# One queue for the first loads, and other priorities and margins for the scheduler of a two-layer decoder trunk

## The chip, the cores and the metric

The kernel runs on one core of a Trainium2 chip (trn2). Five engines work side by side: TensorE (PE in the rows, its weight loads PEld), VectorE (DVE), ScalarE (ACT), GpSimd (POOL) and SyncE (SP, which here only issues DMAs). The metric is the device time of one launch in microseconds (us); lower is better. Three runs of the kernel before took 282.83, 282.81 and 280.10 us, median 282.81 us.

## What is computed

Two layers of a mixer on a residual stream `x` of 256 tokens by 1024 features, all in float32. Cut to what matters:

```python
for l in range(2):
    h = rms_norm(x, g_pre[l]);  u = h @ w_in[l]          # 1024 -> 3344 columns, split into:
    qa, ka, va, ga, qb, kb, vb, gb, rb, qm, gm = split(u)
    oa = causal_attention(norm(qa), norm(ka), va, alibi) * silu(ga)        # 8 heads of 64
    log_a = log_sigmoid(rb @ w_gate_up[l] + b_gate_up[l]) / 16
    ob = rms_norm(gated_linear_attention(qb, kb, vb, log_a)) * silu(gb)    # "GLA", 4 heads, chunks of 64
    mk, mv = split(rms_norm(mem, g_mem[l]) @ w_mem_kv[l])
    om = attention(norm(qm), norm(mk), mv) * silu(gm)                      # 4 heads over 256 memory tokens
    x = x + concat(oa, ob, om) @ w_out[l]
```

## The kernel before

**Numbers in two parts.** A float32 operand is split into a rounded part and a rest (`whi`/`wlo` for weights, `xh`/`xl` for the normalised input, `oh`/`ol` for the gated outputs and, earlier in a layer, for the memory tokens), and each product is three matmuls: high by high, high by low, low by high. The high part is a copy on ACT (line 404 for weights, 345 for the first ones; 259 or, on POOL, 261 for activations), the low part a subtraction on DVE (lines 406, 347, 301).

**Units.** Weights come in granules of 256 columns (1 MB each, 272 columns for `vr`). A layer is a run of units: `vr` and `kq` (what GLA needs), then those of `UNITS[l]` (values, queries and keys, gates, and the memory's `mk`, `mv`), then `o0` to `o3` of the output projection. A unit of one granule is 48 matmuls of 256 columns (line 998); a pair, such as `mk mv`, is 48 of 512 columns (line 1005). These 31 units give 1488 of the 2138 matmuls in the trace, and their order among themselves does not depend on the tables of numbers below. Places on TensorE are told by the count of these big matmuls from the start: `kq` ends at 96, `ga0` at 144, `va0 va1` at 192, `qa0 ka0` at 240, `mk mv` at 288.

**Small work between them.** Between the big matmuls TensorE does transpositions (lines 502, 523, 932), the sums of squares of the norms (438), a broadcast (455) and matmuls that use only a part of the array, "small-tile" work: the gate (530), GLA (686, 692, 614, 621 and, at its end, 732), attention scores (880) and probabilities times values (947). The rests of an attention are on DVE, ACT and POOL: line 482 and 917 are POOL's.

**The order.** Nothing is scheduled on the chip. While the program is built, a planner (`Plan.run`) keeps a clock for each engine; each piece of work is a generator that asks for an engine, a cost, the earliest time and a priority. The planner takes the engine whose next piece could start first, and among the pieces ready on that engine the one of highest priority, and the instructions are written in that order; each engine then works through its list strictly in turn. The big matmuls have priority 0, so small work goes in front of them as soon as the planner's clock says that it is ready. Small-tile work on TensorE is held back by `SLACK` plus `HOLD`:

```python
if eng == "P" and t.mode != "main":
    after += SLACK + (HOLD if t.mode != "full" and self.shape == "full" else 0)
```

**The tables.** `PR` is the priority of each kind of work: `a0`, `a1` the two halves of the causal attention, `m` the memory attention, `v` value evacuations, `qk` query and key evacuations, `vr` the evacuation of the first unit with the gate's chain (`vr_evac`, lines 508 to 545), `gla` the GLA chain, `g` gates. `SPLIT` is the priority of splitting weights that are not yet needed, `MEMPRIO` that of the split of the memory tokens, `FSQ` that of the squares of `x`, `STATS` an extra delay of the matmul of line 438, `WARM` how many matmuls on zeros stand in front of the first real one (line 1035).

**The first loads.** `start_loads` (lines 321 to 338) issues `x` in five pieces and `w0` (the weights of `vr` and `kq`, 528 columns for each of eight k) in five pieces: two of `w0` from ACT's queue, all others from SP's. `LANDS` tells the planner when each piece is there. Behind them come the constants (`cst`), `wup`, and then the other weights, each into one of three raw buffers as one comes free. `first_unit` works through k = 0 to 7, twelve matmuls for each.

## Time and profile before

| | |
|---|---|
| runs | 282.83, 282.81, 280.10 us (median 282.81) |
| the profiled execution | 281.19 us, of which the span (first to last instruction) is 279.4 us |
| TensorE matmul busy | 272.0 us, 97% of the span |
| TensorE weight load busy | 241.1 us, 86% |
| VectorE busy | 229.5 us, 82% |
| ScalarE busy | 193.3 us, 69% |
| GpSimd busy | 89.0 us, 32% |
| chain that ended last | TensorE 87%, VectorE 7%, DMA 2% |

Matmuls overlap one another, so that a row's busy time is longer than the distance from its start to the next start; the distance is what a matmul costs. The chain of work that ended last follows, from the last instruction back, what released each step; its rows add up to the span, and in it a row of matmuls tells the time that passed, not the busy time.

### The profile page before, as it was taken

To read this page: it belongs to the slowest core of one execution; us is meant where nothing else is said; L and a number is where in the kernel's file an instruction comes from. 1 tells how busy PE (TensorE), PEld (TensorE's weight loads), DVE (VectorE), ACT (ScalarE), POOL (GpSimd) and SP (SyncE) were. 2 spreads that over 40 slices of the span, in tenths; PEclk is the share of its full clock that TensorE was granted. 3 is DMA by queue.
4 is the path that set the end of the run, shared out by engine and by line. 5 is a ranking of instruction groups with operands and counts; after the bars stand their busy time and mean duration, and the time that the engine had idled before them with its cause. 6 is when DMAs were issued, how large, how long until landed. Compare 5 with 4: busy or idle time off the path is not lost.

```text
span 279.4 us, 5773 instructions
## 1 busy us (share of the span) xinstructions
PE 272.0 (97%) x2138; PEld 241.1 (86%) x2138; DVE 229.5 (82%) x568; ACT 193.3 (69%) x430; POOL 89.0 (32%) x111
## 2 busy tenths in 40 slices
PE   8899999799999999999999999999999999999994
PEld 7799788487999997999999886789887888989994
DVE  2899799999888898978999798979986787898631
ACT  4874888777797776967773888759787745956400
POOL 3303394160426424400063318213243730510000
PEclk9999999999999999999999999999999999999999
DMA  7999408560734314343545745228233424151111
GB/s 224 402 361 380 175 0 308 198 246 1 289 107 189 103 72 151 122 168 126 201 160 158 287 151 199 104 82 325 63 135 110 192 108 196 50 196 59 56 56 40
DMA packets 8413, 45.76 MB, mean 164 GB/s; under 512 B 945, under 2 KB 2369, under 8 KB 3393
## 3 DMA queue, kind: packets, MB, share of 16 engines
q1 hardware_dynamic: 8096, 44.85, 43.6%
q10 hardware_dynamic: 288, 0.54, 0.7%
q8 instruction: 17, 0.28, 0.4%
q14 instruction: 12, 0.09, 0.1%
HBM read 44.34 MB, written 1.05 MB: 162 GB/s over the span
## 4 chain that ended last, share of the span: by engine, by line
PE 87%; DVE 7%; DMA 2%; ACT 1%; issue 1%
PE bank L998 49%; PE bank L1005 21%; PE bank L947 4%; PE bank L932 3%; PE bank L880 3%; DVE wlo L406 2%; DMA raw<-w_dram 2%; PE bank L502 2%; DVE ol L301 1%; PE bank L732 1%; PE bank L621 1%; DVE sqs L317 1%; ACT L539 0%; PE bank L530 0%; DVE el L581 0%
## 5 line engine op out<-in xcount | busy, mean ns | idle before, releaser
L406 DVE TENSOR_TENSOR wlo<-raw,whi 128x512 fp32r<-128x512 f32 (+1 forms) x144 | 97.8, 700 | 12.0 <-ACT whi L404 10.1
L404 ACT ACTIVATE whi<-raw 128x512 fp32r<-128x512 f32 (+1 forms) x144 | 86.4, 625 | 24.3 <-PE bank L998 11.3
L998 PE MATMUL bank<-xh,whi 128*128 128x256 f32 x160 | 47.1, 294 | 0.0
L998 PE MATMUL bank<-xl,whi 128*128 128x256 f32 x160 | 44.6, 279 | 0.0
L998 PE MATMUL bank<-xh,wlo 128*128 128x256 f32 x160 | 44.6, 279 | 0.0
L917 POOL TENSOR_SCALAR pe<-pe,rc 128x256 f32<-128x256 f32 (+1 forms) x48 | 29.4, 626 | 35.4 <-DVE rc L914 35.2
L998 PE MATMUL bank<-oh,whi 128*128 128x256 f32 x128 | 35.8, 280 | 0.0
L998 PE MATMUL bank<-ol,whi 128*128 128x256 f32 x128 | 35.7, 279 | 0.0
L998 PE MATMUL bank<-oh,wlo 128*128 128x256 f32 x128 | 35.7, 279 | 0.0
L482 POOL TENSOR_TENSOR cc<-ss,nhalf 128x8 f32<-128x8 f32 x12 | 20.5, 1717 | 45.4 <-DVE ss L480 40.9
L1005 PE MATMUL bank<-whi,xh 128*128 128x512 f32 x80 | 32.9, 411 | 0.0
L1005 PE MATMUL bank<-wlo,xh 128*128 128x512 f32 x80 | 31.4, 393 | 0.0
L998 PEld LDWEIGHTS bank<-xh,whi 128*128 128x128 f32 x160 | 30.2, 189 | 1.4 <-issue 1.0
L1005 PE MATMUL bank<-whi,xl 128*128 128x512 f32 x80 | 31.3, 392 | 0.0
L998 PEld LDWEIGHTS bank<-xl,whi 128*128 128x128 f32 x160 | 30.2, 189 | 0.1
L998 PEld LDWEIGHTS bank<-xh,wlo 128*128 128x128 f32 x160 | 30.1, 188 | 0.0
L998 PE MATMUL bank<-whi,xh 128*128 128x256 f32 (+1 forms) x96 | 28.6, 298 | 0.5 <-ACT whi L345 0.5
L998 PE MATMUL bank<-wlo,xh 128*128 128x256 f32 (+1 forms) x96 | 27.6, 288 | 0.5 <-DVE wlo L347 0.4
L998 PE MATMUL bank<-whi,xl 128*128 128x256 f32 (+1 forms) x96 | 27.3, 284 | 0.0
L998 PEld LDWEIGHTS bank<-oh,whi 128*128 128x128 f32 x128 | 24.3, 190 | 0.2 <-issue 0.2
L998 PEld LDWEIGHTS bank<-ol,whi 128*128 128x128 f32 x128 | 24.0, 188 | 0.0
L998 PEld LDWEIGHTS bank<-oh,wlo 128*128 128x128 f32 x128 | 24.0, 188 | 0.0
(188 smaller groups left out, 608.7 us busy)
## 6 DMA issues: line engine op xcount, KB each, us to landing
raw<-win_dram SPq DMA_DIRECT2D x23, 1024.0 KB, 5.3
raw<-wout_dram SPq DMA_DIRECT2D x8, 1024.0 KB, 4.8
raw<-wmkv_dram SPq DMA_DIRECT2D x4, 1024.0 KB, 4.8
raw<-memT_dram SPq DMA_DIRECT2D x2, 1024.0 KB, 4.8
raw<-w_dram SPq DMA_DIRECT2D x3, 528.0 KB, 8.0
raw<-wvr_dram SPq DMA_DIRECT2D x1, 1088.0 KB, 4.9
nb<-nb_dram SPq DMA_DIRECT2D x1, 1024.0 KB, 8.4
out_dram<-xp SPq DMA_DIRECT2D x8, 128.0 KB, 1.9
```

The costliest lines, as they stand in the source:

```text
L301: V.scalar_tensor_tensor(lo[:, k], src[:, k], col(l, g0 + k), hi[:, k].bitcast(F32), op0=ALU.mult, op1=ALU.subtract)
L317: V.tensor_tensor(sqs, sqs, sq[:, j], op=ALU.add)
L404: S.activation(hi[:, cs], raw[:, cs], AF.Copy)
L406: V.tensor_sub(lo[:, cs], raw[:, cs], hi[:, cs].bitcast(F32))
L482: G.tensor_tensor(c, ss, nhalf, op=ALU.pow)
L502: TE.transpose(ps[:, m, tt * P:tt * P + P], n[:, tt, m * P:m * P + P], ident)
L880: TE.matmul(bk[hh][2][:, a:b], lhsT=x[ds], rhs=y[ds], start=(j == 0), stop=(j == len(prs) - 1))
L917: G.tensor_scalar(pe[:, hh, a:b], pe[:, hh, a:b], rc[:, hh, qt:qt + 1], 1.0, op0=ALU.mult, op1=ALU.mult)
L932: TE.transpose(bk[0][2][:, dst:dst + P], pe[:, hh, src:src + P], ident)
L947: TE.matmul(po[64 * hh:64 * hh + 64, q0:T], lhsT=vv[:, j, c:c + 64], rhs=pt[:, hh, 256 * j:256 * j + T - q0], start=(j == 0), stop=(j == 1))
L998: TE.matmul(ps, lhsT=a, rhs=b, start=(first and j == 0), stop=(lastk and j == 2))
L1005: TE.matmul(ps, lhsT=a, rhs=b, start=(first and j == 0), stop=(lastk and j == 2))
```

## The change

The first loads all go to SP's queue, in the order in which `first_unit` uses them (x0, w0, x1, w1, x2-3, w2, w3, x4-5, w4-5, x6-7, w6-7), with six pieces of `w0` where there were five. The dummy matmuls are six where they were five. In the planner the evacuation of the first unit and its gate chain (`vr`) goes from 7 to 9, GLA from 6 to 5, the second half of the causal attention from 8 to 9, the memory attention from 9 to 7, values from 5 to 4, queries and keys from 8 to 7, the split of weights from 6 to 7, the squares of `x` from 6 to 7. `STATS` falls from 800 to 300, `HOLD` rises from 600 to 900. No instruction's kind, shape or engine is changed by hand; the planner makes other lists from these numbers.

```diff
-PR = {'a0': 6, 'a1': 8, 'm': 9, 'v': 5, 'qk': 8, 'vr': 7, 'gla': 6, 'g': 7}
+PR = {'a0': 6, 'a1': 9, 'm': 7, 'v': 4, 'qk': 7, 'vr': 9, 'gla': 5, 'g': 7}
-SPLIT = 6
+SPLIT = 7
-WARM = 5
-FSQ = 6
-STATS = 800
-CHUNKS = ((0, 1), (1, 2), (2, 4), (4, 6), (6, 8))
-LANDS = ((3000, 4200), (4300, 4900), (5600, 6800), (7400, 8500), (9200, 10300))
+WARM = 6
+FSQ = 7
+STATS = 300
+LOADS = (("x", 0, 1, 3100), ("w", 0, 1, 4300), ("x", 1, 2, 4600), ("w", 1, 2, 5300), ("x", 2, 4, 6000),
+         ("w", 2, 3, 6700), ("w", 3, 4, 7600), ("x", 4, 6, 8300), ("w", 4, 6, 9900), ("x", 6, 8, 10600),
+         ("w", 6, 8, 12100))
-SLACK, HOLD = 300.0, 600.0
+SLACK, HOLD = 300.0, 900.0
-        for c, (a, b) in enumerate(CHUNKS):
-            tx, tw = LANDS[c]
-            xs = slice(L * NPRM + a * T if a else 0, L * NPRM + b * T)
-            nc.sync.dma_start(xp[:, xs], xp_d[:, xs])
-            (nc.scalar if b <= 2 else nc.sync).dma_start(raw[:, a:b], src[:, a:b])
-            plan.spawn(first_x(a, b, tx), 30 - 2 * a)
-            plan.spawn(first_w(a, b, tw, raw, hi, lo, got), 29 - 2 * a)
+        for what, a, b, t in LOADS:
+            if what == "x":
+                xs = slice(L * NPRM + a * T if a else 0, L * NPRM + b * T)
+                nc.sync.dma_start(xp[:, xs], xp_d[:, xs])
+                plan.spawn(first_x(a, b, t), 30 - 2 * a)
+            else:
+                nc.sync.dma_start(raw[:, a:b], src[:, a:b])
+                plan.spawn(first_w(a, b, t, raw, hi, lo, got), 29 - 2 * a)
-        yield op("P", 4300, 0.0, None, None, "main")
+        yield op("P", 4700, 0.0, None, None, "main")
```

Line numbers of the changed kernel are one or two higher from line 259 on (998 is 1000, 947 is 949, 261 is 262).

**The start.** SP's list before, from its first DMA (`xp` holds `x` with the parameters in front, `raw` is the first weights' buffer; 528 columns are one k, 264 KB):

```order
L331 DMA xp<-xp_dram 128x302
L331 DMA xp<-xp_dram 128x256
L331 DMA xp<-xp_dram 128x512
L332 DMA raw<-w_dram 128x1056
L331 DMA xp<-xp_dram 128x512
L332 DMA raw<-w_dram 128x1056
```

ACT's list before, at the same place:

```order
L322 ACT_TABLE_LOAD
L322 ACTIVATE warm<-ones 128x1
L332 DMA raw<-w_dram 128x528 x2
L259 ACTIVATE xh<-xp 128x256
L345 ACTIVATE whi<-raw 128x272
```

SP's list now; ACT issues no DMA any more:

```order
L332 DMA xp<-xp_dram 128x302
L335 DMA raw<-w_dram 128x528
L332 DMA xp<-xp_dram 128x256
L335 DMA raw<-w_dram 128x528
L332 DMA xp<-xp_dram 128x512
L335 DMA raw<-w_dram 128x528 x2
L332 DMA xp<-xp_dram 128x512
L335 DMA raw<-w_dram 128x1056
```

The second piece of weights (k = 1) stood on another queue beside SP's x2-3 and w2-3; now it is in front of them on the same queue.

**The memory tokens in layer 0.** TensorE's list before, at the change from the unit `qa0 ka0` (on `xh`) to `mk mv` (on `oh`, which here holds the memory tokens); 679 is GLA's first large matmul, 438 the sum of the memory's squares (`sqs`):

```order
L1005 MATMUL bank_99<-whi,xl 128x512
L679 MATMUL bank_92<-zl_135,ee 128x512
L438 MATMUL bank_94<-ones,sqs_130 128x1 x2
L1005 MATMUL bank_95<-whi,oh 128x512
L1005 MATMUL bank_95<-wlo,oh 128x512
```

And now, twelve big matmuls earlier, still inside `qa0 ka0`, with six of them in front of the GLA matmul:

```order
L1007 MATMUL bank_99<-whi,xl 128x512
L440 MATMUL bank_96<-ones,sqs_130 128x1 x2
L1007 MATMUL bank_98<-whi,xh 128x512
L1007 MATMUL bank_98<-wlo,xh 128x512
L1007 MATMUL bank_98<-whi,xl 128x512
L1007 MATMUL bank_99<-whi,xh 128x512
L1007 MATMUL bank_99<-wlo,xh 128x512
L1007 MATMUL bank_99<-whi,xl 128x512
L681 MATMUL bank_94<-zl_135,ee 128x512
```

POOL's list before, over the same stretch (`oh` is the split of the memory tokens, eight in all; `zl` spreads GLA's `wz` over the heads):

```order
L558 TENSOR_SCALAR qbd<-qf,cst 128x256 x4
L261 TENSOR_SCALAR oh<-raw,xp 128x256 x8
L261 TENSOR_SCALAR zl_135<-wz_133,cst 128x256
L261 TENSOR_SCALAR zl_136<-wz_134,cst 128x384 x2
L445 TENSOR_TENSOR rsx_629<-vx_627,nhalf 128x2
```

And now:

```order
L560 TENSOR_SCALAR qbd<-qf,cst 128x256 x4
L262 TENSOR_SCALAR oh<-raw,xp 128x256
L262 TENSOR_SCALAR zl_135<-wz_133,cst 128x256
L262 TENSOR_SCALAR oh<-raw,xp 128x256
L262 TENSOR_SCALAR zl_135<-wz_133,cst 128x256
L262 TENSOR_SCALAR oh<-raw,xp 128x256 x4
L262 TENSOR_SCALAR zl_136<-wz_134,cst 128x384
L447 TENSOR_TENSOR rsx_603<-vx_601,nhalf 128x2
```

Five of the eight splits of the memory now stand behind a `zl` in POOL's list, and two of the eight have gone to ACT.

**The small-tile work of the attention.** TensorE's list before, in the unit `gb` of layer 1, where the probabilities of the first of two heads' pairs (`pts_125`) are multiplied by the values, and eighteen big matmuls later those of the second (`pts_126`):

```order
L998 MATMUL bank_94<-xl,whi 128x256
L998 MATMUL bank_94<-xh,wlo 128x256
L947 MATMUL bank_99<-pts_125,va_118 64x256 x2
L947 MATMUL bank_99<-pts_125,va_118 64x128 x2
L932 MATMUL bank_98<-cst,pe_124 128x128 x3
L998 MATMUL bank_96<-xh,whi 128x256
L998 MATMUL bank_96<-xl,whi 128x256
```

The second pair's part of that list, after those eighteen:

```order
L998 MATMUL bank_96<-xl,whi 128x256
L998 MATMUL bank_96<-xh,wlo 128x256
L947 MATMUL bank_95<-pts_126,va_118 64x256 x2
L947 MATMUL bank_95<-pts_126,va_118 64x128 x2
L998 MATMUL bank_96<-xh,whi 128x256
```

TensorE's list now, in the same unit:

```order
L934 MATMUL bank_96<-cst,pe_124 128x128 x3
L1000 MATMUL bank_93<-xh,whi 128x256
L1000 MATMUL bank_93<-xl,whi 128x256
L1000 MATMUL bank_93<-xh,wlo 128x256
L1000 MATMUL bank_93<-xh,whi 128x256
L1000 MATMUL bank_93<-xl,whi 128x256
L1000 MATMUL bank_93<-xh,wlo 128x256
L949 MATMUL bank_94<-pts_125,va_118 64x256 x2
L949 MATMUL bank_94<-pts_125,va_118 64x128 x2
L949 MATMUL bank_98<-pts_126,va_118 64x256 x2
L949 MATMUL bank_98<-pts_126,va_118 64x128 x2
```

Two stretches of small-tile work have become one. The same has happened to three such pairs in layer 0.

## Rows read from the trace of the kernel before

**Rows 1.** The page: busy us (share of the span), number of instructions

```profile
span 279.4 us, 5773 instructions
PE 272.0 (97%) x2138; PEld 241.1 (86%) x2138; DVE 229.5 (82%) x568; ACT 193.3 (69%) x430; POOL 89.0 (32%) x111
```

**Rows 2.** Stretches: us, busy of PE, PEld, DVE, ACT, POOL, clock, DMA share, GB/s

```profile
10.00:49.00 39.00, 38.98 (x234) 34.19 (x234) 36.84 (x90) 29.73 (x57) 16.85 (x18) 1.00 0.70 261
49.00:53.00 4.00, 2.30 (x10) 1.12 (x9) 4.00 (x11) 4.00 (x11) 0.48 (x1) 1.00 0.63 246
53.00:276.00 223.00, 222.82 (x1869) 199.13 (x1868) 184.61 (x460) 154.05 (x354) 68.73 (x79) 1.00 0.39 142
```

**Rows 3.** The chain that ended last, at its start: start us, us, what

```profile
1.59 5.94 DMA raw<-w_dram
7.55 0.65 ACT whi L345
8.23 0.80 DVE wlo L347
10.82 8.90 PE bank L998 x71
19.72 0.34 PE bank L438 x4
```

**Rows 4.** TensorE's first matmuls: start us, us, instructions, idle before

```profile
1.17 4.63 PE L1035 MATMUL bank<-ob 128*128 128x256 f32 x10 [1.17 <-DVE ones L1165]
5.83 0.43 PE L998 MATMUL bank<-wlo,xh 128*128 128x272 f32 x1
```

**Rows 5.** Busy by stretch at the start, columns as in rows 2

```profile
6.80:10.00 3.20, 2.30 (x16) 1.89 (x16) 1.77 (x4) 2.43 (x5) 0.71 (x2) 1.00 1.04 391
```

**Rows 6.** TensorE between the units `qa0 ka0` and `mk mv`, columns as in rows 4

```profile
49.10 1.02 PE L679 MATMUL bank<-zl,ee 128*128 128x512 f32 x2
51.16 0.60 PE L438 MATMUL bank<-ones,sqs 128*128 128x1 f32 x4 [1.03 <-DVE sqs L317]
52.76 0.50 PE L1005 MATMUL bank<-wlo,oh 128*128 128x512 f32 x1 [0.67 <-DVE wlo L406]
```

**Rows 7.** The chain where it runs through VectorE, columns as in rows 3

```profile
43.24 0.40 DVE ol L301
48.91 0.20 DVE el L581
50.16 0.60 DVE wlo L406
50.76 0.34 DVE sqs L317
```

**Rows 8.** POOL from the memory's landing on, columns as in rows 4

```profile
34.93 7.51 POOL L261 TENSOR_SCALAR oh<-raw,xp 128x256 fp32r<-128x256 f32 x8 [4.68 <-DMA raw<-memT_dram]
45.47 1.64 POOL L261 TENSOR_SCALAR zl<-wz,cst 128x256 f32<-128x256 f32 x1 [3.04 <-DVE wz L664]
47.68 1.80 POOL L261 TENSOR_SCALAR zl<-wz,cst 128x384 f32<-128x384 f32 x2 [0.57 <-DVE wz L593]
```

**Rows 9.** The chain through small-tile work, columns as in rows 3

```profile
104.22 1.01 PE bank L947 x8
122.47 0.55 PE bank L998 x3
151.04 0.35 PE bank L998 x3
156.65 15.12 PE bank L1005 x66
233.35 1.88 PE bank L947 x16
```

**Rows 10.** VectorE, end of layer 0's last attention, columns as in rows 4

```profile
122.52 0.42 DVE L954 SCALAR_TENSOR_TENSOR of<-bank,ga 128x256 f32<-128x256 f32 x1 [0.30 <-PE bank L947]
123.43 0.42 DVE L852 TENSOR_TENSOR ol<-of,oh 128x256 fp32r<-128x256 f32 x1 [0.15 <-ACT oh L850]
```

More of the change, by code (lines that the diff above doesn't have):

```diff
@@ L327, in start_loads @@
         src = w0_d.rearrange("p (k n) -> p k n", n=NB)
-        for c, (a, b) in enumerate(CHUNKS):
-            tx, tw = LANDS[c]
-            xs = slice(L * NPRM + a * T if a else 0, L * NPRM + b * T)
-            nc.sync.dma_start(xp[:, xs], xp_d[:, xs])
-            (nc.scalar if b <= 2 else nc.sync).dma_start(raw[:, a:b], src[:, a:b])
-            plan.spawn(first_x(a, b, tx), 30 - 2 * a)
-            plan.spawn(first_w(a, b, tw, raw, hi, lo, got), 29 - 2 * a)
+        for what, a, b, t in LOADS:
[6 more added lines that the diff above has]
+                plan.spawn(first_w(a, b, t, raw, hi, lo, got), 29 - 2 * a)
         plan.spawn(first_sq(), 5)
         nc.sync.dma_start(cst, cst_d)
-        cst_ev.set(12300)
+        cst_ev.set(12800)
         nc.sync.dma_start(wup, wup_d)
```

## The prediction

> **What bounds the kernel now.** I read the page's busy times first: TensorE's matmuls are busy for 97% of a span of 279.4 us, VectorE for 82% [rows 1]. Such a share is a mean, so the next view is the busy time by stretch [rows 2]. From 10 to 49 us and from 53 to 276 us TensorE has no idle time to speak of (222.82 of 223.00 us). It lacks work only in the first 10 us, in a hole between 49 and 53 us (2.30 of 4.00), and in the last 3.4 us, which the change does not touch. VectorE, on the other hand, is full in the hole (4.00 of 4.00) and has 2.2 us to spare in the 39 us before it. So a change of order can win in three ways: a better start, a smaller hole, and cheaper work in the long full stretches.
>
> **The start.** The chain begins with one DMA, the weights of k = 1: 264 KB, issued on ACT's queue at 1.59 us, took 5.94 us [rows 3], because SP's 256 and 528 KB for k = 2 and 3 moved beside it. Behind it stand ACT's split (0.65) and VectorE's (0.80), and from 10.82 us TensorE runs 71 matmuls in 8.90 us, 0.125 each, up to 19.72, where 96 are done [rows 3]. The dummy matmuls fill 1.17 to about 5.8 us, and the second real matmul starts at 5.83 [rows 4]. Now k = 1's weights are fourth on the only queue, with 151 + 264 + 128 KB ahead. From 1.59 us on, these 807 KB need 2.1 us at the 391 GB/s of 6.8 to 10 us [rows 5], 3.1 us at the 261 of the later stretch [rows 2]: by about 4.7 us, say 5.5 with what lies between the last byte and the signal. The sixth dummy is two more of the ten in the trace, 4.63 / 10 = 0.46 or a little less each, so the second real matmul moves to 5.83 + 0.85 = 6.7 us. k = 1 is then wanted at 6.7 + 11 x 0.125 = 8.1 us, and its weights must have landed by 8.1 - 0.65 - 0.80 = 6.6 us: a margin of 1 us in the worse case. From there on a k is 392 KB, 1.0 us at 391 GB/s, against 1.5 us of matmuls; ACT and VectorE have kept that pace already in the 71. So the other 94 matmuls end at 6.7 + 94 x 0.125 = 18.5 us instead of 19.72. **Gain 1.2 us**; between a loss of 0.9 (the dummies alone, nothing won by the order) and a gain of 1.4 (a little more if the 94 go at the 0.35 / 3 = 0.117 us of later ones [rows 9], less the k of 272 columns among them). The matmul of line 438 (0.34) now stands before the last six of these 96 instead of behind them, which moves it and costs nothing; its squares end on VectorE at about the time at which they did, less the same 1.2 us.
>
> **The hole.** Before, GLA's matmul of line 679 starts at 49.10, then line 438 waits 1.03 us for VectorE's last sum of the memory's squares, and the first `wlo` of `mk mv` is 0.67 us late [rows 6]: 1.7 us. Now line 438 stands twelve big matmuls earlier. At 15.12 / 66 = 0.229 us each [rows 9] that is 49.10 - 2.75 = 46.35, and with the start's gain TensorE gets there at 45.15. When is VectorE ready? Its last sum of squares ended at 51.10 [rows 7]. In the two lists, eight instructions that stood before it now stand behind it: two `wlo` (0.60 each), a split of the memory (0.40) and five of GLA's (0.20) [rows 7], 2.6 us. That gives 48.5; VectorE follows TensorE's start, 1.2 us earlier, 47.3; and the gate's chain, now at priority 9, may use up the 2.2 us in which it idled, 45.1. So the wait is 0 to 2.1 us by this account. The second account goes by POOL, for five of the memory's splits now stand behind a `zl`, which needs VectorE's `wz`. Behind `wz` come two `zl` at 1.64 us (0.90 if they go like the two later ones) and four splits at 7.51 / 8 = 0.94 [rows 8], then 1.5 us on VectorE: `wz` + 8.5. `wz` ended just before 45.47 [rows 8]; twelve instructions less stand ahead of it in VectorE's list now (six splits of the memory, two `wlo`, three sums of squares, one of GLA's: 5.0 us), so it ends at 45.4 - 5.0 - 1.2 = 39.2, or 37.0 with the idle time used: ready at 45.5 to 47.7, a wait of 0.3 to 2.5 us. I take 0.9 us, nearer the lower ends, since the `zl` were slow where VectorE was full and the idle time was the gate chain's. **Gain 1.7 - 0.9 = 0.8 us**, between -0.8 and 1.7. What is late next is GLA's second group of levels (line 621), which moves from matmul 282 to 267 and so asks VectorE for its factors sooner; the 2.5 us hold a wait there too.
>
> **The merged stretches.** Four pairs of stretches at line 947 become four single ones (three in layer 0, one in layer 1), by `HOLD` and the new priorities. Three big matmuls behind such a stretch take 0.55 us and three elsewhere 0.35 [rows 9]: 0.20 for leaving and entering. Two stretches in one take 1.88 us where one takes 1.01 [rows 9]: 0.14 less than twice. 4 x (0.20 + 0.14) = **1.4 us gain**; at least 4 x 0.20 = 0.8. The other shapes, scores next to values inside one stretch, change as often as before (seven times). Against this term stands that matmuls are busy there for 222.82 of 223.00 us [rows 2]; if that were the bound, the sum below would be 279.2. But 0.55 and 0.35 are distances from start to start inside that same stretch, so the time is there to be won. The Trainium skill's "Trainium Kernel Development and Optimization", section Performance Expectations, says the same of the busy row: matmul busy time is a bad measure of how near a kernel is to its bound, since matmuls are pipelined, and weight-load busy time is a better one. By that rule the term stays and the sum is 277.8; the weight loads' 199.13 us of the same 223 [rows 2] agree with it.
>
> **Everything else at nothing.** The lists of VectorE, ACT and POOL hold the same work, and ACT the same nine table loads. What now comes later (values, the memory's attention, GLA's end) is covered by big matmuls: the last values of layer 0 stand 18 of them, 2.1 us, before the output projection reads them, while the chain behind them took from 122.52 to 123.85, 1.3 us [rows 10], and the two of the merged stretch need 0.8 more on VectorE. If that cover were gone, each late 0.1 us would be paid once in a layer.
>
> **The sum.** 281.19 - 1.2 - 0.8 - 1.4 = **277.8 us**, against the profiled execution's own time (span 279.4 and 1.8 around it). The timed runs lie from 1.1 us below that to 1.6 above, median 282.81, so a median of the changed kernel may lie as far off.
>
> **The rivals.**
> - *VectorE's backlog stays.* It is full from the memory's landing to the hole, and the start's gain makes TensorE ask sooner. For it: both accounts reach over 2 us. Against: 2.6 us less work stands ahead. The wait is then 1.7 to 2.5: 281.19 - 1.2 - 1.4 + 0 to 0.8 = 278.6 to 279.4.
> - *The start wins nothing.* k = 1's weights come after 6.6 us, or the dummies eat what the order wins. For it: no row has the rate of one queue alone in the first 5 us. Against: the margin of 1 us is reckoned at the lower of two rates. 281.19 + 0.9 - 0.8 - 1.4 = 279.9 at worst, 279.0 at half.
> - *The merges win nothing*, because TensorE is full: 279.2, as worked out above. Against: the 0.55 and 0.35.
> - *Slower: POOL's list.* If GLA's `wz` is late, five memory splits wait behind a `zl` that waits for it, VectorE's sums stand behind those splits, and line 438 stops all of TensorE. With `wz` at its old 45.4 us the sums end at 53.9, a wait of 8.8 us: 281.19 - 1.2 - 1.4 - 1.7 + 8.8 = 285.7. It decides from a `wz` at 45.15 - 8.5 + 4.3 = 40.9 us. Against: 5.0 us less work ahead of it.
>
> **How the numbers follow.** The forecast case has 0.55: a start between 0.9 and 1.4, a wait in the hole under 1.7, merges between 0.8 and 1.4, which gives 276.7 to 278.5 by themselves. The backlog has 0.24, the start 0.10, the merges 0.05, POOL 0.06. One per cent, 2.8 us, is about what a measurement of this kernel can tell from no change: from 278.4 to 284.0. Of the first case nearly all lies below that, and a little of the others: faster 0.57, same 0.37, slower 0.06. The range reaches from 275.6 (the best sum, 276.7, less the 1.1 by which a run can lie below the profile) to 280.6 (the backlog and the start cases, some way up towards the median's 1.6), and leaves out about 2 in 10.
>
> **What would show each step.** The start: the 96 big matmuls of `vr` and `kq` end near 18.9 us with the 0.4 of line 440 among them, and no idle gap above 0.3 us after the dummies. The hole: line 440 of the memory starts at 45 to 46.5 us, and TensorE's idle time from 40 to 62 us is under 1 us; if it is near 2, the backlog is right; if VectorE's sums wait for POOL's `oh`, the fourth rival's mechanism is. The merges: 0.55 for three matmuls behind four fewer stretches, and the time from there to the end of the span shorter by 1.4. The forecast is wrong if a wait appears where I have none: at the output projection behind the merged values of layer 0, or at line 621.

## The result, and the profile after

The changed kernel takes 279.54 us (median of 15 runs, 278.05 to 280.03) against 281.25 us (15 runs, 280.10 to 282.83): a ratio of 0.9938, interval 0.9918 to 0.9959. The median is 1.71 us or 0.6% lower: half of the 3.4 us forecast, inside the range, but short of the one per cent that the prediction's likeliest outcome (faster, 0.57) asks for. The two profiled executions stand 281.19 to 279.74, the spans 279.4 to 278.0.

The page's busy times after, and the stretches in the columns of [rows 2]:

```profile
span 278.0 us, 5780 instructions
PE 271.7 (98%) x2140; PEld 241.6 (87%) x2140; DVE 228.3 (82%) x571; ACT 192.6 (69%) x429; POOL 92.6 (33%) x109
```

```profile
10.00:49.00 39.00, 38.65 (x228) 33.26 (x227) 36.91 (x96) 30.18 (x58) 16.82 (x17) 1.00 0.73 276
49.00:53.00 4.00, 4.00 (x69) 2.93 (x68) 3.74 (x10) 3.33 (x7) 3.98 (x1) 1.00 0.40 164
53.00:276.00 223.00, 220.48 (x1809) 197.97 (x1807) 182.47 (x455) 152.45 (x354) 68.73 (x78) 1.00 0.39 143
```

The hole at 49 to 53 us is gone (4.00 busy, 2.30 in [rows 2]), and the long stretch, which had 0.18 us of idle time, now has 2.5. Of these 1.6 lie past the last matmul, which ends near 274.4 us; the other 0.9 are idle time inside the work. The waits of TensorE behind the dummies name most of it (us in total, times, longest):

```profile
PE bank L504 <- DVE nh L491: 0.8, 2, 0.6
PE bank L440 <- DVE sqs L318: 0.3, 1, 0.3
PE bank L1000 <- DVE wlo L349: 0.3, 1, 0.3
```

Before, line 438 (now 440) waited 1.03 us and the `wlo` behind it 0.67 [rows 6]. Now 440 waits 0.35, and line 504, the transposition of `qa0`'s normalised heads at big matmul 273, waits 0.56 and 0.20. TensorE's rows there (start us, us, instructions, idle before):

```profile
45.96 0.61 PE L440 MATMUL bank<-ones,sqs 128*128 128x1 f32 x4 [0.35 <-DVE sqs L318]
61.94 0.33 PE L504 MATMUL bank<-cst,nh 128*128 128x128 f32 x1 [0.56 <-DVE nh L491]
62.47 0.55 PE L504 MATMUL bank<-cst,nh 128*128 128x128 f32 x3 [0.20 <-DVE nh L491]
```

The start, as the chain that ended last has it (answer to [rows 3]):

```profile
3.03 5.05 DMA raw<-w_dram
...
9.55 8.59 PE bank L1000 x65
18.14 0.34 PE bank L440 x4
```

The DMA at the head is now that of k = 2, no longer of k = 1; its `wlo` is the one that line 1000 waits 0.3 us for. Six more big matmuls follow line 440. Measured at the same instruction, the 97th big matmul starts at 19.14 us instead of 19.92. Line 438 (now 440) stands ahead of it in both lists; from the 98th on, when what follows its small matmuls has passed too, TensorE is 0.87 us ahead.

### The profile page after: what moved, and what is told of

It is laid out like the page before. It is cut to its first block, busy times and chain, and to the rows that moved or that the text cites. A ratio compares the mean times of both kernels' runs of the same rounds, so it can differ in the third digit from the quotient of the medians.

```text
span 278.0 us, 5780 instructions
## 1 busy us (share of the span) xinstructions
PE 271.7 (98%) x2140; PEld 241.6 (87%) x2140; DVE 228.3 (82%) x571; ACT 192.6 (69%) x429; POOL 92.6 (33%) x109
## 3 DMA queue, kind: packets, MB, share of 16 engines
HBM read 44.34 MB, written 1.05 MB: 163 GB/s over the span
## 4 chain that ended last, share of the span: by engine, by line
PE 78%; DVE 11%; DMA 4%; POOL 2%; ACT 1%; issue 1%; SPq 1%; POOLq 0%
PE bank L1000 45%; PE bank L1007 17%; DVE wlo L408 4%; PE bank L949 4%; PE bank L934 3%; PE bank L882 3%; DMA raw<-memT_dram 3%; PE bank L504 2%; DMA raw<-w_dram 2%; POOL cc L484 1%; PE bank L734 1%; DVE ol L302 1%; DVE sqs L318 1%; DVE ss L475 1%; ACT pe L899 1%
## 5 line engine op out<-in xcount | busy, mean ns | idle before, releaser
L1000 PE MATMUL bank<-xh,whi 128*128 128x256 f32 x160 | 46.5, 291 | 0.0
L484 POOL TENSOR_TENSOR cc<-ss,nhalf 128x8 f32<-128x8 f32 x12 | 21.5, 1800 | 40.4 <-DVE ss L482 40.4
L1000 PEld LDWEIGHTS bank<-oh,wlo 128*128 128x128 f32 x128 | 24.6, 192 | 0.0
```

What stands on the lines that cost most here:

```text
L484: G.tensor_tensor(c, ss, nhalf, op=ALU.pow)
L1000: TE.matmul(ps, lhsT=a, rhs=b, start=(first and j == 0), stop=(lastk and j == 2))
```

## The experiments

The runs were measured in three sets, each with the kernel before beside them (medians 281.51, 281.62 and 281.41 us); each ratio is against "before" of its own set. Places are numbers of big matmuls, and "ahead" or "behind" compares the starts of the same big matmul in two traces.

**The loads alone.** Two kernels take the loads' order without the numbers. e1_queue puts all on SP's queue and keeps the pieces; e7_single also issues k = 2 and k = 3 one by one.

```diff
-            (nc.scalar if b <= 2 else nc.sync).dma_start(raw[:, a:b], src[:, a:b])
+            nc.sync.dma_start(raw[:, a:b], src[:, a:b])                   # e1_queue
+            for k0, k1 in ((2, 3), (3, 4)) if a == 2 else ((a, b),):       # e7_single
+                nc.sync.dma_start(raw[:, k0:k1], src[:, k0:k1])
```

> The kernel before, with one word changed: the weights of k = 0 and 1 are issued on SP's queue, between the inputs, and not on ACT's. The planner does not see queues, so the lists of TensorE, VectorE, ACT and POOL stay as they were, dummies included (five). Theory (the start was bound by the weights of k = 1, which moved beside 784 KB that are wanted later): they land about 1.5 us sooner, near 6.1 us; the big matmuls of vr and kq end 1.2 us sooner, near 18.5 us instead of 19.72; and the whole is 0.8 to 1.4 us shorter. Rival A (VectorE's backlog takes it back): the same start, but line 438 and the first wlo of mk mv wait longer by what was won, 1.7 us becoming 2.5 or more, and the whole is shorter by less than 0.4 us. Rival B (the queue's order is not what delayed k = 1): the 96 matmuls end within 0.3 us of 19.72 and the time is the same.

> The kernel before with all first loads on SP's queue, as in the run before, and besides the weights of k = 2 and of k = 3 as two DMAs of 264 KB and not one of 528. The lists of TensorE, VectorE, ACT and POOL stay as in the kernel before, with five dummies. Theory (with the queue in order the start is bound by the weights of k = 2, which in one DMA with k = 3 land at 9.35 us): they land near 8.2, and the 96 big matmuls end near 18.6 us instead of 19.9, 1.2 us sooner. For the whole there are two answers: if TensorE's wait in the hole is fixed by its distance from the start, the whole is 1.2 us shorter; if VectorE's backlog fixes the time of the hole, line 438 and the first wlo of mk mv wait 1.2 us longer than their 1.7, and the whole stays within 0.4 us of before. Rival (k = 2 is not it either): the 96 end within 0.3 us of before.

Measured: 281.57 us, ratio 1.0004 (0.9978 to 1.0029), and 281.57 us, 0.9999 (0.9973 to 1.0026): no gain from either. The chain at the start of e1 is:

```profile
3.03 6.31 DMA raw<-w_dram
...
10.80 8.90 PE bank L998 x71
```

k = 1 lands at 6.35 us there, in good time, but the pair k = 2 and 3 lands at 9.35, and TensorE's 71 matmuls start at 10.80, as before (10.82): the next piece was the bound at once. In e7 k = 2 lands alone at 7.53, the 71 start at 9.61, and the 97th big matmul at 18.93 instead of 19.92. That single pieces give this gain isn't shown, though: e12, further down, has the loads of before and its 97th at 18.91. The whole time of e7 does not move either. In its trace the hole shows where the gain went (columns of [rows 2]):

```profile
48.00:50.00 2.00, 1.13 (x4) 0.26 (x2) 2.00 (x7) 2.00 (x6) 0.61 (x1) 1.00 0.76 287
50.00:52.00 2.00, 1.06 (x6) 0.75 (x6) 2.00 (x6) 2.00 (x6) 0.00 (x0) 0.95 0.48 201
52.00:54.00 2.00, 2.00 (x5) 1.37 (x5) 2.00 (x5) 1.09 (x3) 0.71 (x1) 0.50 0.22 41
54.00:56.00 2.00, 2.00 (x25) 0.97 (x26) 1.94 (x7) 0.00 (x0) 0.29 (x1) 0.69 0.93 385
```

VectorE is full (2.00 of 2.00), and TensorE idles 0.87 and 0.94. That is 1.81 us, with 1.70 in before, so the hole moved along with the start. But behind it the granted clock falls to 0.50, 1.2 of 2.4 GHz, from 51.8 to 55.2 us, and a lead of 0.88 us at the 240th big matmul is a lag of 0.60 at the 258th. The four executions of e7 without such a fall have median 280.74, those of before 280.50, so they win nothing either; how early before starts in most of its executions no trace tells.

**The numbers alone.** e2_prio is before with the changed `PR`, `SPLIT`, `FSQ`, `STATS` and `HOLD`, and the old loads.

> The kernel before with the other half of the change alone: the new priorities, HOLD 900, STATS 300; the loads, their times and the five dummies stay. In its order three stretches of small-tile work fewer stand than before (21 for 24), line 438 of the memory stands at big matmul 225, and the transpositions of the first two head norms at 276 and 282. If the terms add up (merges 0.34 each, the hole 1.7 less a rest of about 0.5, the start nothing, the new wait at the transpositions up to 1.1): 3 x 0.34 + 1.2 - 0 to 1.1 = 1.1 to 2.2 us shorter than before. Rival (the loads alone carry the gain, and the priorities give back at the transpositions what they win in the hole): within 0.5 us of before. Layer 1, which has the same order as the changed kernel, should take the same time as there, 0.6 us less than before.

Measured: 283.3 us, ratio 1.0058 (1.0032 to 1.0083): slower by 1.8 us, where the theory had it 1.1 to 2.2 faster and the rival within 0.5. TensorE's wait, POOL's list and the stretch behind (columns of [rows 2]):

```profile
52.88 1.16 PE L679 MATMUL bank<-zl,ee 128*128 128x512 f32 x2 [2.68 <-POOL zl L261]
```

```profile
48.32 4.03 POOL L445 TENSOR_TENSOR rsx<-vx,nhalf 128x2 f32<-128x2 f32 x1
52.35 1.60 POOL L261 TENSOR_SCALAR zl<-wz,cst 128x256 f32<-128x256 f32 x3
```

```profile
54.00:56.00 2.00, 2.00 (x8) 0.80 (x6) 1.92 (x4) 0.00 (x0) 0.00 (x0) 0.50 0.00 0
```

GLA's line 679 waits 2.68 us for a `zl` on POOL, which stands behind the memory's `rsx`, a power of 128 by 2 numbers that took 4.03 us. This is the fourth rival's mechanism, a late piece in POOL's list that stops TensorE, at another place of the list. The changed kernel has the same power at 48.94 us, 4.04 long, but with that `zl` ahead of it. From the 224th to the 266th big matmul e2 loses 3.1 us against before, part of it at half clock (53.8 to 57.3 us). Its three executions without such a fall take 281.90 to 282.61, so most of the loss is there without it. Neither half of the change gains anything alone (0.9999 and 1.0058); together they give 0.9938. The effects don't add.

**The clock.** Of the 65 executions of the kernel before in the three sets, 39 have a mean granted clock of 0.994 or less, and their median is 282.03 us; 26 have 1.000 and 280.50. Of 21 of the changed kernel none is under 0.997, and such a small loss need not cost anything: in e8's trace, with 0.999, the clock falls at 276.1 us, behind the last matmul. The profiled execution of before is one of the undisturbed ones, so its rows show nothing of this. The theory: idle time in the hole sometimes brings the half clock that e7 shows, and the change, which breaks the hole up, is rid of it. e12_fill keeps the kernel before and fills the hole with two dummies:

```diff
+        if out is mrs_ev:
+            for j in range(FILL):                                  # 2
+                TE.matmul(ps[:, 0:256], lhsT=zero[:, 0:128], rhs=zero, start=True, stop=True)
         for tt in range(2):
```

> The kernel before with two dummy matmuls of 256 columns (0.43 us each, as those at the start) put ahead of the memory's line 438, where TensorE waits 1.03 us for VectorE's sums. Lists of the other engines stay. Theory (in about half of the executions of the kernel before, the 1.7 us in which TensorE lacks work in the hole are followed by some 3.4 us at half the granted clock, as the traces of two kernels here show at 52 to 57 us, with 0.994 as the mean of the execution): with the hole mostly filled no execution has a mean clock of 0.994, the dummies cost nothing, and the median comes down by 0.5 to 0.9 us against before. Rival (the clock falls for another reason): as many executions at 0.994 as in before, and the same median.

Measured: 280.61 us against 281.41, ratio 0.9979 (0.9955 to 1.0002), and none of 12 executions at 0.994 or less (0.997 to 1.000). TensorE there:

```profile
48.95 1.02 PE L440 MATMUL bank<-ob 128*128 128x256 f32 x4
50.25 0.61 PE L442 MATMUL bank<-ones,sqs 128*128 128x1 f32 x4 [0.28 <-DVE sqs L318]
51.85 0.50 PE L1009 MATMUL bank<-wlo,oh 128*128 128x512 f32 x1 [0.67 <-DVE wlo L407]
```

The wait of 1.03 is 0.28 with the dummies in it, and nothing starts sooner by them: this trace is 1.01 us ahead of before's at the 97th big matmul, 0.94 at the end. That the fall hangs on this hole is shown by the counts (39 of 65 against 0 of 12); on the time alone the interval still reaches 1, and 280.61 is what the undisturbed executions of before take (280.50).

**The changed kernel again.** e11_again is the changed kernel word for word.

> The changed kernel once more, word for word. It tells whether the pace of the long runs belongs to the program or to the execution. If to the program: the output projections of both layers go at 117.8 ns again, and the spans of its executions lie as close as those of the other kernels. If to the execution: one of the two projections goes at 113.3 in this trace, the position of the layer boundary is 0.85 us earlier for the first, and the time lies 0.9 us under the first trace for each.

Measured: 278.83 us, ratio 0.9904 (0.987 to 0.9938), lower than the 279.54 of the first set; the 21 executions together have median 279.35. Its trace has no wait at line 504. Busy time from 40 to 62 us, before, after, and e11:

```profile
40.00:62.00 22.00, 20.30 (x140) 15.52 (x139) 21.36 (x60) 17.79 (x38) 10.93 (x10) 1.00 0.65 239
```

```profile
40.00:62.00 22.00, 21.05 (x185) 15.71 (x183) 19.77 (x56) 15.49 (x32) 15.66 (x10) 1.00 0.60 226
```

```profile
40.00:62.00 22.00, 21.65 (x191) 16.50 (x190) 20.68 (x57) 15.68 (x33) 15.04 (x10) 1.00 0.62 231
```

Idle time from 40 to 62 us is 1.70, 0.95 and 0.35 us. The difference between the last two sits on POOL, in the power of line 484 that turns `qa0`'s sums of squares into factors (after, then e11):

```profile
58.32 4.71 POOL L484 TENSOR_TENSOR cc<-ss,nhalf 128x8 f32<-128x8 f32 x2 [0.90 <-DVE ss L482]
```

```profile
58.11 3.27 POOL L484 TENSOR_TENSOR cc<-ss,nhalf 128x8 f32<-128x8 f32 x2 [0.90 <-DVE ss L482]
```

Two of them take 4.71 us in one execution and 3.27 in the other; of the twelve in a launch the median is 1.647 us in both, the longest 3.107 in after and 2.069 in e11. Nor is the long one a single case: this power takes 3.107, 3.106, 3.111 and 3.107 us in after, e4, e5 and e8, whose lists are the same up to here, and TensorE waits 0.55 and 0.20 us at the transposition in all four. e11 is the exception. In e8:

```profile
58.03 4.71 POOL L506 TENSOR_TENSOR cc<-ss,nhalf 128x8 f32<-128x8 f32 x2 [0.89 <-DVE ss L504]
```

In after it began at 58.32, beside a close run of VectorE:

```profile
58.36 0.15 DVE L482 TENSOR_TENSOR ss<-ss,evx 128x8 f32<-128x8 f32 x1
58.44 0.68 DVE L408 TENSOR_TENSOR wlo<-raw,whi 128x512 fp32r<-128x512 f32 x1
59.24 0.68 DVE L408 TENSOR_TENSOR wlo<-raw,whi 128x512 fp32r<-128x512 f32 x1
61.46 0.42 DVE L491 TENSOR_TENSOR nh<-bank,cc 128x256 f32<-128x256 f32 x1 [1.54 <-POOL cc L484]
```

In e11 the same small addition stands beside it:

```profile
58.15 0.21 DVE L482 TENSOR_TENSOR ss<-ss,evx 128x8 f32<-128x8 f32 x1
```

VectorE's run ended at 59.92 and the power at 61.43, 1.51 us later, a little less than one takes undisturbed; in e4, e5 and e8 these are 1.51 us too. The power of 128 by 2 numbers does the same: in nine traces, e2's among them, it takes 4.03 to 4.04 us, in e6 1.42, and in all ten it ends 0.57 us after a two-input instruction of VectorE (a `wlo` or an `el`). The Trainium skill's "SBUF — State Buffer", section "SBUF: two separate sides", says that VectorE (with two inputs from SBUF) and GpSimd share a pair of ports which one of them holds for a whole instruction while the other waits. These times agree with that. Which of the two gets in seems a matter of tens of ns: in after the addition starts 39 ns behind the power and takes its usual 0.155 us, in e11 it starts 41 ns behind and takes 0.208, and there the power goes through in 1.667 us. What decides isn't settled.

**The new wait.** Three kernels act on line 504's wait. In e3_later the order is frozen and the transpositions stand nine (the second four: three) big matmuls later, with VectorE's reads of them:

```diff
 TensorE
-L504 MATMUL bank<-cst,nh 128x128 x4
 L1007 MATMUL ... x9
+L504 MATMUL bank<-cst,nh 128x128 x4
```

> The changed kernel with its whole order of work written out as a table and not planned, and in that table one thing moved: TensorE's transpositions of the first two head norms (line 504, for qa0 and ka0) stand nine and three big matmuls later, with what reads them behind them. Everything else keeps its place. Theory (the hole moved there: these transpositions came when VectorE's nh was not ready, and stopped TensorE for 1.1 us): the wait goes, nothing else waits longer, and the time is 1.0 to 1.2 us below the changed kernel, 2.7 to 2.9 below the one before. Rival A (VectorE has no time to spare there, so the wait moves on to the scores at line 882 or to the next wlo): the time stays within 0.4 us of the changed kernel, and a new wait of about 1 us stands between 64 and 72 us. Rival B (TensorE falls into another pace behind the moved rows): the wait goes, but the total moves by another 0.4 to 0.9 us either way in the output projections, whose rows are untouched.

Measured: 279.99 us, 0.9936 (0.991 to 0.9962): no gain over the changed kernel (279.35 for its 21 executions), and a new wait where rival A has it. There is none at 504, but in this trace the power took 1.67 us as in e11, so the move need not be the reason. Big matmul 288 comes 1.67 us earlier than in after's trace; by 336 all but 0.03 of that is gone, at the attention's values, whose line is 756 here:

```profile
68.47 1.52 PE L756 MATMUL bank<-att,vb 128*64 128x256 f32 x16 [1.09 <-DVE att L286]
```

The wait moved on to VectorE's next late piece. e9_first takes the other side, and brings the sums of `qa0` forward in VectorE's list:

```diff
 VectorE
-L408 TENSOR_TENSOR wlo<-raw,whi 128x512 x2
-L475 TENSOR_REDUCE ss<-sq 128x8
 L475 TENSOR_REDUCE ss<-sq 128x8
 L482 TENSOR_TENSOR ss<-ss,evx 128x8
+L408 TENSOR_TENSOR wlo<-raw,whi 128x512 x2
+L475 TENSOR_REDUCE ss<-sq 128x8
```

> The changed kernel with its order of work as a table; in VectorE's list two instructions move: the sum of squares of the head norm of qa0 and its small addition (lines 475 and 482) stand ahead of two wlo of mk and mv, and not behind them and the sum of ka0. Nothing else moves, on no engine. Theory (in the changed kernel VectorE waited 1.54 us for POOL's pow before it could make nh, because the sum that feeds POOL came 1.3 us later than it could): POOL starts about 0.9 us sooner, nh is there before TensorE comes to line 504, the waits of 1.15 us there go, and the time is 0.9 to 1.2 us below the changed kernel. Rival A (the two wlo are wanted at once): TensorE waits at the big matmuls 264 and following for wlo by 0.5 us or more, and the gain is under 0.5 us. Rival B (the wait moves on to GLA's line 734 or to the scores, as in the run in which line 504 stood later): the time stays within 0.3 us.

Measured: 280.51 us, 0.9953 (0.9925 to 0.998), slower than the changed kernel's 278.83 of the same set. That theory fell, and neither rival had it slower. ACT's rows, e9 and then after:

```profile
62.65 1.16 ACT L428 ACTIVATE whi<-raw 128x512 fp32r<-128x512 f32 x2 [4.03 <-DMA raw<-win_dram]
```

```profile
61.07 1.15 ACT L406 ACTIVATE whi<-raw 128x512 fp32r<-128x512 f32 x2 [2.28 <-DMA raw<-win_dram]
```

The two `wlo` that moved back are the last readers of a raw buffer. The next weights' DMA into it is issued at 57.52 us instead of 56.09, and ACT waits 4.03 us for it instead of 2.28. VectorE's next `wlo` waits 2.10 us for ACT's copy (63.31 us), and the second head norm's `nh`, which stand behind it in VectorE's list, come at 64.92 and 65.64 us instead of 63.96 and 64.69. TensorE, 0.75 us ahead of after's trace at the 284th big matmul, waits for them (0.36 and 0.39 us) and is 0.44 behind at the next; another 0.45 go at the norm at GLA's end, and at the 336th it is 0.98 behind. e6_less relieves VectorE itself:

```diff
+SKIP = ((0, "mk", 4), (0, "mv", 4), (0, "qm", 0))
+            if (l, nm, a) not in SKIP:
                 V.tensor_sub(lo[:, cs], raw[:, cs], hi[:, cs].bitcast(F32))
```

> The changed kernel with its order of work kept, and three VectorE instructions left out (the low halves wlo of one quarter each of the weights mk, mv and qm of layer 0; their old contents are used instead, so the output isn't the reference's). They stand in VectorE's list between 51 and 57 us, ahead of the head norms whose transpositions stop TensorE at 61 us, and take 0.6 us each, 1.8 in all. Theory (from the memory's landing to 72 us VectorE is the bound, and TensorE's waits there are VectorE's backlog, wherever they fall): line 504 waits less by all of its 1.15 us, and no new wait takes its place; the time is 1.1 to 1.5 us below the changed kernel. Rival A (the wait is POOL's, whose two pow of 1.6 us each stand in the chain): VectorE is done sooner but line 504 still waits 0.6 us or more, and the time is at most 0.6 us less. Rival B (the next thing is late at once, GLA's levels or the scores): the wait moves on, as in the run in which line 504 stood later, and the time stays within 0.3 us.

Measured: 278.17 us, 0.9875 (0.9846 to 0.9904), six runs within 0.5 us. Its row for 40 to 62 us:

```profile
40.00:62.00 22.00, 21.72 (x191) 16.68 (x191) 19.54 (x54) 16.01 (x33) 12.69 (x10) 1.00 0.62 239
```

With 1.8 us less on VectorE TensorE is busy for 21.72 of 22.00 in this stretch, where only line 440's 0.3 is left of its waits, and big matmul 336 comes 1.60 us before after's. But here too the power was short (1.90 us): 1.0 of the 1.6 is what e11 has with all of VectorE's work, so less work brings 0.6, a third of the 1.8. Moving a piece (e3, e9) brought nothing; taking work away brought a part; an undisturbed power brought more than either.

**The merges.** e8_apart takes two of the merged stretches of line 949 apart again, one in each layer, the order frozen otherwise:

```diff
 TensorE, layer 1
 L949 MATMUL bank<-pts,va 64x128 x2
-L949 MATMUL bank<-pts,va 64x256 x2
-L949 MATMUL bank<-pts,va 64x128 x2
 L1000 MATMUL ... x18
+L949 MATMUL bank<-pts,va 64x256 x2
+L949 MATMUL bank<-pts,va 64x128 x2
```

> The changed kernel with its order of work as a table, in which two of the merged stretches are pulled apart again: in layer 1 the values of the second pair of heads (line 949) stand eighteen big matmuls behind those of the first, in layer 0 the memory's second values eighteen behind the scores. What follows them on other engines moves with them; all else stays. Theory (a stretch more costs 0.34 us, 0.10 of it when TensorE returns to full tiles and the rest when it leaves them and in a shorter stretch): the rest of layer 0 starts 0.3 us later from there, that of layer 1 0.3 to 0.4 us more, 0.65 us in all, if the paces of the runs behind are the same. Rival (TensorE is full either way and merging wins nothing): under 0.2 us at each of the two places.

Measured: 279.23 us, 0.9912 (0.9881 to 0.9943). By the starts of the next big matmuls each place loses 0.30 us against after (layer 1: from 0.64 to 0.33 ahead of it; layer 0: from 0.27 ahead to 0.03 behind), where the prediction had 0.34. The chain in layer 1, after and then e8:

```profile
246.27 1.45 PE bank L949 x16
```

```profile
245.63 0.80 PE bank L971 x8
246.43 2.32 PE bank L1022 x18
248.75 0.80 PE bank L971 x8
```

Two stretches of 0.80 stand for one of 1.45. The whole kernel did not get 0.6 us slower, though, and the reason is the next point.

**Two paces.** A run of 256-column big matmuls, at the full clock and with nothing else in between, has one of two steady distances from start to start, 113.3 or 117.8 ns to within 0.4, in all traces here. A run settles on one of them in its first four to six matmuls and keeps it to its end, for 186 and 225 matmuls in the changed kernel's two longest runs. Busy time from 124 to 140 us, in layer 0's output projection, for before, after, e11 and e8:

```profile
124.00:140.00 16.00, 16.00 (x144) 16.00 (x143) 13.43 (x28) 11.62 (x24) 0.00 (x0) 1.00 0.52 188
```

```profile
124.00:140.00 16.00, 16.00 (x138) 16.00 (x137) 13.85 (x29) 11.06 (x23) 0.00 (x0) 1.00 0.46 163
```

```profile
124.00:140.00 16.00, 16.00 (x138) 16.00 (x137) 13.76 (x30) 11.51 (x25) 0.04 (x1) 1.00 0.43 145
```

```profile
124.00:140.00 16.00, 16.00 (x144) 16.00 (x143) 13.83 (x29) 11.25 (x24) 0.00 (x0) 1.00 0.49 169
```

TensorE is 16.00 of 16.00 busy in all four, and issues 144 matmuls or 138. Before is fast in layer 0 and slow in layer 1, and so are e1, e7 and e12, whose lists are the same there; the changed kernel is slow in both, and so are e11, e6 and e9; e8 is fast in both. For these two long runs the pace belongs to the program. It need not for a shorter one: the 45 matmuls from the 330th on go fast in after, e5 and e11, slow in e4 and e8. Layer 1, before, after and e8, as the chain has it:

```profile
249.49 26.36 PE bank L998 x222
```

```profile
247.72 26.71 PE bank L1000 x225
```

```profile
249.55 23.70 PE bank L1022 x207
```

That is 0.119, 0.119 and 0.114 us each. 192 matmuls by 4.5 ns are 0.86 us for each layer: from the 600th big matmul to the end of layer 0's projection the change lost 0.74 of it, and e8 has the fast pace in both layers. To test this apart from any order, e4_cuts and e5_pace write one matmul of a run as two halves, which shifts the rhythm at its start and leaves all else:

```diff
+            if cut and j == 1:
+                TE.matmul(ps[:, :cut], lhsT=a, rhs=b[:, :cut], start=False, stop=False)
+                TE.matmul(ps[:, cut:], lhsT=a, rhs=b[:, cut:], start=False, stop=False)
+                continue
```

> The changed kernel with the same order of work; only in the output projections the second big matmul of each group of 48 is issued as two, of so many columns and of the rest: in layer 0 cut at 64, 96, 128 and 160 columns, in layer 1 at 128, 32, 192 and 80. The sums computed are the same. Each cut costs a weight load and some 0.1 us. Theory (TensorE has two steady paces for the same 256-column matmul, 113.3 and 117.8 ns from start to start, and what happens in the first few matmuls of a run decides which one it keeps): some of the eight groups run at 113.3 behind their cut, others at 117.8, and each of the first kind is 0.21 us shorter less the cut's 0.1. Rival (the pace belongs to the place, by what the other engines or the DMA queues do then, or by the banks used): all four groups of a layer stay at 117.8 as in the changed kernel, and the time is 0.4 to 0.8 us longer by the cuts alone.

> The changed kernel with its order of work kept; eight of its 256-column big matmuls are issued in two halves of 128 columns: one near the start of each of eight long runs of such matmuls that went at 117.8 ns in the trace of the changed kernel (the numbers of the big matmuls are 291, 309, 375, 429, 582, 846, 999 and 1263; the runs behind them hold 15, 21, 18, 72, 186, 18, 18 and 224). Theory (two paces, and a cut sends a run into the fast one, as in all eight groups of the run before): these 572 matmuls go at 113.3, which is 572 x 4.5 ns = 2.6 us less, minus eight cuts at about 0.07: the time is 2.0 us below the changed kernel, near 277.4 us, and the runs scatter less. Rival (it was chance that eight of eight went fast): about half of the runs turn, and the time is 0.5 to 1.2 us below the changed kernel.

Measured: e4, with a cut at the head of each of the eight groups of the output projections, 278.88 us, 0.9895 (0.9864 to 0.9926); e5, with cuts of 128 columns at eight other places, 278.85 us, 0.99 (0.9868 to 0.9933), where the theory had 277.4. In e4 all eight groups run fast behind the cut, in e5 six of eight. A cut costs about 0.11 us (distances of 61, 113 and 171 ns stand where two of 118 stood), so a group of 48 matmuls, which gains 0.2, nets 0.1. One cut for a whole projection should then pay better. e10_both is e9 with one cut in each layer, at big matmuls 582 and 1263, so that it reads against e9:

> The run with the head norm's sum moved ahead, and besides two cuts of a 256-column big matmul into halves, at the big matmuls 582 and 1263, where the two longest runs begin (186 and 224 matmuls, at 117.8 ns in the trace of the changed kernel). Theory: 410 x 4.5 ns = 1.85 us less, minus two cuts at 0.165 as the run with eight cuts showed: 1.5 us, together with the 0.9 to 1.2 of the move 2.4 to 2.7 us below the changed kernel, near 277.0 us. Rival (paces change from execution to execution, so the changed kernel has the fast one in many of them already): only 0.5 to 0.9 us below the run with the move alone.

Measured: 278.92 us, 0.9909 (0.9877 to 0.9942), against e9's 280.51 of the same set: 1.59 us less, 1.54 by the traces from big matmul 582 on. Layer 0 and layer 1 of e10:

```profile
124.00:140.00 16.00, 16.00 (x143) 16.00 (x142) 14.07 (x29) 11.01 (x23) 0.00 (x0) 1.00 0.50 184
```

```profile
248.35 25.36 PE bank L1030 x223
```

143 for 138, and 0.114 each. The pace is real, it is set at the head of a run, and two cuts turn it. What in the rhythm of the first matmuls decides isn't settled: widths of 32 to 192 columns all did it in e4, 128 failed at two places in e5. None of e4, e5, e8 and e10 is faster than e11, the changed kernel itself (278.83), beyond the spread; e10's two cuts on the changed kernel without e9's move were not run.

## Why the prediction held only half its gain

The places at which time could be won were read rightly. What each was worth can be read at big matmuls before which both lists have done the same work, so that the rows add up to the difference of the two spans:

| stretch (big matmuls) | term | forecast | measured |
|---|---|---|---|
| to the 110th | the start | -1.2 | -0.87 |
| 110th to 392nd | the hole and what is late next | -0.8 | +0.02 |
| 392nd to 600th | three merges, layer 0 | -1.05 | -0.70 |
| 600th to 797th | everything else: layer 0's output projection | 0 | +0.74 |
| 797th to the end | one merge, layer 1, and the rest | -0.35 | -0.63 |
| | sum | -3.4 | -1.44 |

The pace changed in the other stretches too: their 256-column matmuls stand 1.6 ns closer from the 110th to the 392nd, 0.8 wider in the third row, and 0.3 closer in layer 1 ahead of its projection. Without that, by an estimate from these distances, the hole reads +0.2, the four merges -1.4 together, and the pace +0.6 in all.

**The start was smaller than its term, and varies more.** k = 1 landed at 6.08 us, inside the 6.6 that it had, and the second real matmul came at 6.19, ahead of the 6.7; but then k = 2's `wlo` was late, and TensorE lost some 0.5 us. Besides, the 19.72 from which the term was reckoned is the end of the 96th matmul by the chain, while 18.5 counts from start to start, where it is 19.56. And the row behind it all, 5.94 us for k = 1, is one execution's. The same DMA of the same loads takes 4.99 us in e12:

```profile
1.59 4.99 DMA raw<-w_dram
...
9.81 8.90 PE bank L1002 x71
```

Its 71 matmuls start at 9.81 instead of 10.82 with no change to the loads at all. The 97th big matmul starts at 19.92, 19.67 and 18.91 us in the three traces with the old loads (before, e2, e12), and between 18.65 and 19.28 in the nine with the new ones: from 1.3 us of gain to 0.4 of loss, about 0.5 by the means. The prediction took a duration that varies for a constant.

**The hole: the step "what is late next" failed.** The account of line 440 was right: at 45.96 us (45 to 46.5 forecast) with a wait of 0.35 (0.9 taken, from 0 to 2.5 reckoned). Nor did VectorE's sums wait for POOL: it works without a gap from 39 to 46 us. From the 227th big matmul to the 266th the change wins 1.62 us, nearly all of the 1.7. It gives 1.45 back by the 287th. What was late next was named as line 621; now at 623, it is 0.25 us late. The larger one was not named: line 504 (0.73 and 0.42 beyond the usual distance), behind POOL's power of 3.107 us. By the 392nd another 0.2 go at the norm at GLA's end, lines 748 and 749 (0.40 late). The first rival, VectorE's backlog, gives 278.6 to 279.4 and so comes near the time, but its mechanism, a wait of 1.7 to 2.5 us at line 440, did not occur.

The prediction took each POOL piece at the time that it had in before's rows, and did not ask what VectorE would run beside it at its new place. In e11, where the power is short, the transposition finds its input ready 0.3 us ahead, about as in before (0.4), and this term comes to -0.87, what was forecast. Against e12, which has e11's start but the old order, e11's span is 1.51 us shorter.

**The merges were right**, about by size too: four of them, 0.30 measured each in the two places where they were pulled apart. The rival that they win nothing because TensorE is busy for 222.82 of 223.00 us is out. What the Trainium skill's "Trainium Kernel Development and Optimization", section Performance Expectations, says of the matmul row agrees: 1.3 us were won in the third and the last stretch, out of a row that was full.

**"Everything else at nothing" failed** by 0.74 us in layer 0's output projection: the same matmuls in the same order ran at 117.8 ns in place of 113.3. The prediction had both distances before it, in 0.117 us from one row and others near it, and took them for one.

**What no step had: the clock.** Medians of before contain its falls to half clock, which the one profiled execution doesn't show. Undisturbed executions of both kernels are 280.50 - 279.35 = 1.15 us apart, those of before with and without the fall 282.03 - 280.50 = 1.53. How much of the 1.71 of the first set comes from such falls is not known, for no clock of its executions of before is on record but the profiled one's. The prediction put its own spread at that of before's three runs; the changed kernel's 21 executions lie between 278.0 and 280.0 us, those of before between 280.1 and 282.8 in the first set alone.

**The range and the chances.** The bounds of the forecast case (a start of at least 0.9, any gain in the hole, merges of at least 0.8) reach 281.19 - 0.9 - 0.8 = 279.5 at their upper end, not 278.5, so that "nearly all lies below" 278.4 and the 0.57 for faster were too high. That 279.54 lies in the range is in part luck: its upper part was drawn for the backlog and a lost start, and it was filled by a held-up power and a slower pace.

The signs that would have shown the forecast wrong, a wait behind the merged values of layer 0 or one that counts at line 621, did not come; the sign for the hole, idle time from 40 to 62 us under 1 us, did (0.95), while the loss stood in distances rather than in idle time.

## What to carry to other kernels

When a stall is filled by moving work forward, ask for each moved piece what the other engines will run beside it at its new place: its duration there need not be the one that it had. Before a term is drawn from one row, compare it with that row in other executions, and look at the clock of all executions and not only of the profiled one. Account for a change at places where both programs have done the same work, so that the terms add up to the whole. Check the steady distance between equal matmuls in each long run: two programs can differ by 4% there with the same instructions in the same order.

## What the runs showed of the hardware

- A 256-column matmul of rounded float32 goes at 113.3 or 117.8 ns, settled at the head of a run and kept; a matmul cut in two at the head (0.11 us) turned 14 of 16 runs in e4 and e5, and both in e10.
- In the kernel before 39 of 65 executions have a mean granted clock of 0.994 or less, 26 have 1.000; with the gap of 1.03 us filled by dummies none of 12 has 0.994 or less. In the traces of e7 and e2 the half clock follows that hole (51.8 to 55.2 and 53.8 to 57.3 us), after idle times of 0.87 and 0.94 in e7 and 2.68 in e2.
- A power on POOL of 128 by 8 numbers took 1.65 us as a rule (up to 2.08 at some places), and 3.11 in four traces beside a close run of VectorE, where it ended 1.51 us after that run; one of 128 by 2 took 0.71, 1.42 and 4.03 us, and where it took 1.42 or 4.03 it ended 0.57 us after a two-input instruction of VectorE.
- The same DMA of 264 KB, issued at 1.59 us beside the same others, took 5.94 us in one execution and 4.99 in another.
- Two subtractions moved back in VectorE's list delayed a DMA by 1.4 us, since they were the last readers of the buffer.
